# Four modulation vectors of the first block as row products on VectorE, and all later modulation issued after the first two heads' projections

## The chip, the core and the metric

The kernel runs on one core of one Trainium2 chip. A core has TensorE (PE, the matrix engine; its weight loads are PEld), VectorE (DVE), ScalarE (ACT), GpSimd (POOL) and SyncE (SP), which here issues most of the DMAs. Each engine works through its own instructions in order; engines wait for one another through semaphores. The metric is the device time of one execution in microseconds (us), as the median of the runs.

## The reference, cut to what matters

One transformer block with three mixers and a mixture of experts, then a second block of two layers. What the change touches is the modulation of the first block: `c` is one vector of 1024 numbers, and a 1024 x 6144 matrix turns it into six vectors.

```python
def first_block(x, c, ctx, c_ctx, w_mod, b_mod, ...):
    sc  = jax.nn.silu(c)                                  # (1, 1024)
    scc = jax.nn.silu(c_ctx)[None]
    mod_x = (sc @ w_mod + b_mod).reshape(-1, 6, 1024)     # six vectors for x
    mod_c = (scc @ w_mod[:, :2048] + b_mod[:2048])        # two for the context
    hx = modulate(rms_norm(x, g_mix), mod_x[:, 0], mod_x[:, 1])
    hc = modulate(rms_norm(ctx, g_mix), mod_c[0], mod_c[1])
    mx = hybrid_mixer(hx, hc, ...)                        # retention, window, neighbourhood
    x = x + mod_x[:, 2] * mx
    hx = modulate(rms_norm(x, g_ffn), mod_x[:, 3], mod_x[:, 4])
    x = x + mod_x[:, 5] * expert_choice_ffn(hx, ...)
# second_block: for each of two layers three more vectors, silu(c_2) @ mod_w_2[l] + mod_b_2[l],
# for x and for the context
```

Vectors 0 and 1 are wanted at once, 2 to 5 only behind the mixer. The vectors of the second block do not depend on the first and can be computed at any time.

## The kernel before

Activations lie as 128 channels by 512 tokens (256 for the context), eight tiles `hx` or `hc` for 1024 channels. A projection (`proj`) loads one 512 KB weight tile `wr` on SP's queue, splits it into a high part `wh` (a cast on ACT, L395) and a rest `wl` (a subtraction on DVE, L391), and multiplies three times (L404 to L406) over eight chunks, 24 matmuls in all. There are two buffers for `wr` and three each for `wh` and `wl`.

A modulation (`modblock`) goes in steps: a step loads a 512 KB tile `wm` and multiplies it by the silu vector, a stationary operand of 32 columns, with two matmuls of 512 columns (L471). 2048 columns take 16 steps; then four transposes (L480) turn the row into columns and DVE adds the bias (L486). `wmod0` (vectors 0 and 1) is drained at the start. `wmod1` and `wmod2` (vectors 2 to 5) and the second block's `mw1a` and `mw1b` (`mods2`, `mods2g`; 16 and 8 steps) follow through the generator `mods`, whose steps `pace` puts between those of the projections: one step for every PACE[i] units of projection cost, a projection being 5.2.

The stretch that the change touches is `block1_mixer` from the first retention projection on. `ret_proj(0)` projects heads 0 and 1 (four q and k projections with a rotary embedding on DVE, then the context's k, `v` for tokens and context, two gates). After its first projection the context `c` is loaded, squared and summed, and `hc` is normed and modulated. `ret_consts` computes the decay constants (`ls`, 24 tiny DVE instructions in a chain, then `lgs`). `ret_attn` makes for each head a strip `G` and a strip `CG` from them (`ret_strips`) and then goes over six key blocks: scores on PE, times the strip on DVE (the tile `A`, L832), `A` times v on PE (L834, L837). While it runs, `weave` fills in `ret_proj(1)` and later the first merge gates `G(0, 10)`, both with `mods` paced in. `drain(mods)` issues what is left, and the window attention follows.

The order on each engine is fixed when the kernel is built: a scheduler goes by the program order, the dependencies and its own idea of durations. Pools give the buffers: the tag `wbig` of pool `mr` has `s.nbig` buffers for modulation weights.

Of the kernel before, what the change touches and what calls it, by code (L numbers as in the profile page):

```python
# [7 lines left out]
F32 = mybir.dt.float32  # L8
# [7 lines left out]
D = 1024  # L16
# [127 lines left out]
def prep(i):  # L144
    f = {k: np.asarray(v) for k, v in i.items()}
    o = dict(_constants())
    o["xT"] = _tokT(f["x"][0])
    o["cT"] = _tokT(f["ctx"][0])
    o["cc"] = np.ascontiguousarray(np.stack([_cols(f["c"][0]), _cols(f["c_ctx"])], axis=-1))
    m = _modchunks(f["w_mod"][0])  # L150
    for n, a in enumerate(m):
        o[f"wmod{n}"] = a
    o["bmod"] = _cols(f["b_mod"][0])
    o["gmix"] = _cols(f["g_mix"][0])
    o["gffn"] = _cols(f["g_ffn"][0])
    o["gfin"] = _cols(f["g_final"])
    w = f["w_in"][0]
    off = {}
    at = 0
    for n, s in (("q_r", 512), ("k_r", 512), ("v_r", 512), ("g_r", 512), ("q_w", 512), ("k_w", 128), ("v_w", 128),  # L160
                 ("q_n", 512), ("k_n", 512), ("v_n", 512), ("gates", 3072)):
        off[n] = (at, s)
        at += s
    order = []

    def cols(n, a, m):
        return w[:, off[n][0] + a:off[n][0] + a + m]

    for h in (0, 256):
        order += [_tiles(cols(n, h, 256)) for n in ("q_r", "k_r")]  # L170
        order += [_vtiles(cols("v_r", h, 256)), _tiles(cols("g_r", h, 256))]
    order += [_tiles(cols("k_w", 0, 256)), _tiles(cols("q_w", 0, 512))]
    for h in (0, 256):
        order += [_tiles(np.concatenate([cols("q_n", h, 128), cols("k_n", h, 128)], axis=1)),
                  _vtiles(cols("v_n", h, 256)),
                  _tiles(np.concatenate([cols("q_n", h + 128, 128), cols("k_n", h + 128, 128)], axis=1))]
    order.append(_tiles(cols("gates", 0, 3072)))
    o["win"] = np.concatenate(order)
    o["lgt"] = _bcast(f["ret_decay_logit"][0])
    o["gn"] = _cols(f["ret_gn"][0])  # L180
    o["sink"] = _bcast(f["win_sink"][0])
    o["wbr"] = np.concatenate([_tiles(f["w_ret"][0]), _tiles(f["w_win"][0]), _tiles(f["w_na"][0])])
    o["wout"] = _tiles(f["w_out"][0])
    o["wrt"] = np.concatenate([f["w_router"][0], np.zeros((D, 16), np.float32)], axis=1).reshape(8, 128, 32).transpose(1, 0, 2)

    wg, wu, wd = [f[n][0].reshape(8, 2, 2, 4, 128, 2, 512).transpose(0, 5, 2, 1, 4, 3, 6)
                  for n in ("w_exp_gate", "w_exp_up", "w_exp_down")]
    o["wexp"] = np.concatenate([np.stack([wg, wu], axis=2).reshape(8, 16, 128, 2048), wd.reshape(8, 8, 128, 2048)],
                               axis=1)
    idx, ok = _na_index()  # L190
    rpb = f["na_rpb"][0]
    o["nab"] = np.stack([np.where(g[None], rpb[:, a[0], a[1]], np.float32(NEG)) for a, g in zip(idx, ok)], axis=1)
    _prep2(f, o)
    return {k: np.ascontiguousarray(v) for k, v in o.items()}
# [40 lines left out]
def drain(g):  # L235

    while True:
        try:
            next(g)
        except StopIteration as e:  # L240
            return e.value
# [40 lines left out]
def pace(main, extra, every):  # L282

    due = 0.0
    for c in main:
        yield c
        due += c
        while due >= every:
            due -= every
            c = next(extra, None)  # L290
            if c is not None:
                yield c
# [25 lines left out]
class Kern:  # L318
# [141 lines left out]
    def modblock(s, sc, src, width, dst, bias, col0, big=None, ps=None):  # L460

        nc = s.nc
        ps = s.mm() if ps is None else ps
        nj = width // 512
        for k in range(8):
            for j in range(nj):
                if j % 2 == 0:
                    w = s.wp.tile([128, 1024], F32, name=s.uid("wr"), tag="wraw", bufs=NRAW) if big is None else \
                        big.tile([128, 1024], F32, name=s.uid("wm"), tag="wbig", bufs=s.nbig)
                    nc.sync.dma_start(w, src[k][:, j * 512:j * 512 + 1024])  # L470
                nc.tensor.matmul(ps[32 * j:32 * j + 32, :], sc[:, k, :], w[:, j % 2 * 512:j % 2 * 512 + 512],  # L471
                                 start=k == 0, stop=k == 7)
                if j % 2:
                    yield 0.9
        n = 32 * nj
        rows = s.T(nm="mrow", tag="t5")
        nc.scalar.copy(rows[:n], ps[:n])
        pt = s.at()
        for i in range(4):
            nc.tensor.transpose(pt[:, i * 128:i * 128 + n], rows[:n, i * 128:i * 128 + 128],  # L480
                                s.const("ident")[:n, :n])
        pv = pt.rearrange("p (i j v) -> p j i v", i=4, j=4)
        for v in range(2):
            o = dst[:, v, col0:col0 + 4 * nj].rearrange("p (j i) -> p j i", j=nj)
            b = bias[:, col0:col0 + 4 * nj].rearrange("p (j i) -> p j i", j=nj)
            nc.vector.tensor_tensor(o, pv[:, 0:nj, :, v], b, ALU.add)  # L486
        yield 0.5


    def rstd_c(s, sq_sum, n, width, fold=None):  # L490
# [594 lines left out]
    def block1_mixer(s, xd, M, ctx2):  # L1085
# [18 lines left out]
        R = [{}, {}]  # L1104
        Y = []
        with s.pool("rp") as s.rp, s.pool("mr") as mr:
            s.nbig = 3
            pm = s.sc()
            bk = [pm[:, i * 512:i * 512 + 512] for i in range(3)]
            mods = itertools.chain(s.modblock(sc, s.d["wmod1"], 2048, mod, bm, 16, mr, bk[0]),  # L1110
                                   s.modblock(sc, s.d["wmod2"], 2048, mod, bm, 32, mr, bk[1]),
                                   s.mods2(1, M[1], mr, bk[2]), s.mods2g(1, M[1], mr, bk[0]))
            s.rdl, s.rcos, s.rsin = [s.pconst(s.rp, n) for n in ("dl", "cosr", "sinr")]
            g = s.ret_proj(0, R[0])
            next(g)
            c = s.loadx("cT", 256, "pj")
            qc = s.sqsum(c, 256)
            for _ in range(3):
                next(g)
                next(mods)  # L1120
            s.sc2 = s.silu2("cc2")
            rc = s.rstd_sb(qc, D, 256)
            s.hc = s.normmod(c, 256, A1[:, 1, :], mod[:, 1, 0:8], lambda: s.TT(256, "hc", "hc"), rc)
            drain(pace(g, mods, PACE[0]))
            s.ret_consts()
            fill.add(pace(s.ret_proj(1, R[1]), mods, PACE[1]))
            weave(s.ret_attn(0, R[0], Y), fill, 2.4)
            fill.flush()
            fill.add(pace(G(0, 10), mods, PACE[2]))
            weave(s.ret_attn(1, R[1], Y), fill, 1.8)  # L1130
            drain(mods)
# [965 lines left out]
    return {a: b if isinstance(b, (tuple, str)) else (b, w) for a, b in k.items()}  # L2097


PACE = (2, 2.5, 2.5)  # L2100
NEARLY = 20
NPRE = 44
LATE = True
# [98 lines left out]
```

## Time and profile before

| | us |
|---|---|
| median of 3 runs | 2881.63 (2880.66 to 2888.18) |
| the profiled execution, its own time | 2883.79 |
| its span, first to last instruction | 2882.0 |
| PE busy | 2717.6 (94%) |
| DVE busy | 1569.0 (54%) |
| ACT busy | 1230.7 (43%) |
| POOL busy | 144.5 (5%) |

How to read it: the span is that of the profiled execution; its own time is 1.8 us longer, and 2.2 us above the median. A share of busy time is a mean over stages. The change lies in the first 330 us, so that stretch is read by windows (busy time of each engine in a stretch), by the timeline (instructions in order of time, with the idle time before them and what ended it) and by the tiles concerned.

### The profile page before, as it was taken

Reading aid. Unit: us, or ns where it says so; the run is one execution under the profiler, and the core shown is the slowest. Engines: PE = TensorE matmul, PEld = TensorE weight load, DVE = VectorE, ACT = ScalarE, POOL = GpSimd, SP = SyncE. Lnnn points to the kernel's source line nnn. Section 1 sums busy time; section 2 is a strip of 40 time slices with the busy share of each in tenths; the row PEclk is TensorE's granted clock in tenths of the full one; section 3 lists DMA queues with packets and bytes.
Section 4 is the critical chain, followed back from the end, with each engine's and each line's share of the span. In section 5 each row is a group of like instructions: output and inputs, shape, how many; then the busy total and the mean of one; then the engine's idle time right before and its main releaser. Section 6 shows DMA issues by size and latency. Waiting matters only on the chain. (4 is left out here: it accounts for less than half of the span.)

```text
span 2882.0 us, 42045 instructions
## 1 busy us (share of the span) xinstructions
PE 2717.6 (94%) x16470; PEld 1889.2 (66%) x16470; DVE 1569.0 (54%) x2957; ACT 1230.7 (43%) x2159; POOL 144.5 (5%) x228
## 2 busy tenths in 40 slices
PE   6999999899969999999999899999999999989998
PEld 3666677787623555555555577777777777767776
DVE  3554676665442323455223656546866546746864
ACT  2333454354222214455212444445655544545652
POOL 1000001000001000000000000000010000000000
PEclk9999999999969999999999999999999999999998
DMA  8545425535789898888999532214354432114343
GB/s 281 174 168 183 145 77 178 189 103 198 263 315 356 304 331 295 316 286 295 321 331 333 189 113 78 72 39 141 115 181 135 131 116 89 50 34 140 117 159 120
DMA packets 170022, 537.68 MB, mean 187 GB/s; under 512 B 21784, under 2 KB 24936, under 8 KB 169824
## 3 DMA queue, kind: packets, MB, share of 16 engines
q1 hardware_dynamic: 141600, 462.50, 46.2%
q0 software_dynamic: 16128, 50.48, 5.3%
q10 hardware_dynamic: 12096, 22.03, 2.1%
q8 instruction: 129, 2.11, 0.3%
q14 instruction: 69, 0.57, 0.1%
HBM read 484.06 MB, written 48.76 MB: 185 GB/s over the span
## 5 line engine op out<-in xcount | busy, mean ns | idle before, releaser
L391 DVE TENSOR_TENSOR wl<-wr,wh 128x1024 fp32r<-128x1024 f32 x320 | 390.9, 1223 | 367.9 <-ACT wh L395 348.8
L395 ACT CAST wh<-wr 128x1024 fp32r<-128x1024 f32 x320 | 334.1, 1046 | 435.0 <-PE ps L405 355.0
L404 PE MATMUL ps<-hx,wh 128*128 128x512 f32 x1168 | 474.9, 407 | 12.8 <-ACT wh L395 7.7
L405 PE MATMUL ps<-hx,wh 128*128 128x512 f32 x1168 | 467.8, 401 | 0.0
L406 PE MATMUL ps<-hx,wl 128*128 128x512 f32 x1168 | 466.3, 400 | 0.6 <-DVE wl L391 0.5
L1301 PE MATMUL ps<-we,xe 128*64 128x512 f32 x1024 | 293.0, 609 | 5.0 <-DMA we<-in_wexp 4.9
L404 PEld LDWEIGHTS ps<-hx,wh 128*128 128x128 f32 x1168 | 221.4, 190 | 76.8 <-issue 12.4
L406 PEld LDWEIGHTS ps<-hx,wl 128*128 128x128 f32 x1168 | 220.9, 189 | 53.5 <-issue 5.0
L405 PEld LDWEIGHTS ps<-hx,wh 128*128 128x128 f32 x1168 | 221.4, 190 | 50.8 <-issue 6.4
L673 ACT ACTIVATE P<-ps,st 128x768 f32<-128x768 f32 (+3 forms) x144 | 111.0, 771 | 148.4 <-DVE st L669 113.6
L1301 PEld LDWEIGHTS ps<-we,xe 128*64 128x64 f32 x1024 | 77.8, 137 | 133.8 <-issue 107.8
L404 PE MATMUL ps<-hc,wh 128*128 128x256 f32 x496 | 145.1, 293 | 3.6 <-ACT wh L395 3.4
L406 PE MATMUL ps<-hc,wl 128*128 128x256 f32 x496 | 144.1, 291 | 0.2 <-DVE wl L391 0.2
L1301 PE MATMUL ps<-we,hT 128*64 128x512 f32 x512 | 139.9, 601 | 2.1 <-ACT hT L1341 1.6
L405 PE MATMUL ps<-hc,wh 128*128 128x256 f32 x496 | 140.2, 283 | 0.0
L667 DVE TENSOR_REDUCE st<-ps 128x1 f32<-128x768 f32 (+3 forms) x144 | 114.1, 793 | 40.7 <-PE ps L406 38.5
L695 PE MATMUL ps<-c_ident,P 128*128 128x128 f32 x688 | 112.0, 283 | 13.2 <-DVE P L678 6.4
L406 PEld LDWEIGHTS ps<-hc,wl 128*128 128x128 f32 x496 | 94.2, 190 | 28.2 <-issue 12.2
L695 PEld LDWEIGHTS ps<-c_ident,P 128*128 128x128 f32 x688 | 81.8, 143 | 46.8 <-ACT PT L698 14.2
L404 PEld LDWEIGHTS ps<-hc,wh 128*128 128x128 f32 x496 | 94.4, 191 | 26.8 <-issue 15.1
L698 ACT COPY PT<-ps 128x512 f32<-128x512 f32 x123 | 70.1, 586 | 88.5 <-PE ps L695 88.0
L471 PE MATMUL ps<-wm,sc_cc 128*32 128x512 f32 x384 | 88.1, 646 | 16.5 <-DMA wm<-in_wmod 16.5
(515 smaller groups left out, 5058.4 us busy)
## 6 DMA issues: line engine op xcount, KB each, us to landing
we<-in_wexp SPq DMA_DIRECT2D x384, 512.0 KB, 7.4
wr<-in_win SPq DMA_DIRECT2D x240, 512.0 KB, 3.8
wm<-in_wmod SPq DMA_DIRECT2D x48, 512.0 KB, 5.3
wr<-in_wbr SPq DMA_DIRECT2D x48, 512.0 KB, 3.5
dram<-th ACTq DMA_DIRECT2D x72, 256.0 KB, 2.1
mth<-dram SPq DMA_DIRECT2D x72, 256.0 KB, 5.0
wr<-in_wout SPq DMA_DIRECT2D x32, 512.0 KB, 4.2
dram<-mth POOLq DMA_DIRECT2D x48, 256.0 KB, 3.0
```

Source lines behind the costliest of these rows:

```text
L391: s.nc.vector.tensor_tensor(out, a, b, ALU.subtract)
L395: i = s.nc.scalar.copy(hi, src)
L404: t.matmul(out, a[0], b[0], start=start, stop=False)
L405: t.matmul(out, a[0], b[1], start=False, stop=False)
L406: t.matmul(out, a[1], b[0], start=False, stop=stop)
L471: nc.tensor.matmul(ps[32 * j:32 * j + 32, :], sc[:, k, :], w[:, j % 2 * 512:j % 2 * 512 + 512], start=k == 0, stop=k == 7)
L667: nc.vector.tensor_reduce(st[:, 0:1], sc[:, :n], AX.X, ALU.max)
L673: nc.scalar.activation(p[:, :n], sc[:, :n], AF.Exp, bias=st[:, 1:2], scale=scale, accum_out=st[:, 2:3])
L695: nc.tensor.transpose(tp[:, j:j + 128], blocks[(i + j) // 128], s.const("ident"))
L698: nc.scalar.copy(parts[i // 512][:, :m], tp[:, :m])
L1301: nc.tensor.matmul(ps[64 * e:64 * e + 64, :], stat[:, k, 64 * e:64 * e + 64], ws[e][:, kk * 512:kk * 512 + 512], start=k == 0, stop=k == 7)
```

## The change

- `prep` hands over `wmod1` and `wmod2` transposed as `wmodT`: 32 tiles of 128 output channels by 1024 inputs, the same bytes in the same number of DMAs. `crow` is `c` repeated over 128 partitions (512 KB).
- `silu_row` loads `crow` into a tile `row` on POOL's queue and takes twice its silu in place: two tanh on ACT, two `scalar_tensor_tensor` on DVE, each 128x512.
- `modrows` takes the place of the two `modblock`s: for each of the 32 tiles one DMA on SP's queue and one `scalar_tensor_tensor` on DVE of 128x1024, which multiplies the weight tile by 0.5 and by the row and sums along the row (`accum_out`) into one column of `mod`. One addition of the bias ends it. TensorE has no part in it.
- In `ret_proj(0)` no modulation is paced any more. The chain `mods` (row products, then `mods2`, `mods2g`) and the second block's `silu2` are issued behind it and behind `ret_consts`.
- `mr` has two `wbig` buffers instead of three, since `row` takes the room of one. PACE goes from (2, 2.5, 2.5) to (0, 1.8, 1.8).

```diff
@@ prep
-    for n, a in enumerate(m):
-        o[f"wmod{n}"] = a
+    o["wmod0"] = m[0]
+
+    o["wmodT"] = f["w_mod"][0][:, 2048:].T.reshape(32, 128, D)
+    o["crow"] = _bcast(f["c"][0])
@@ class Kern
+    def silu_row(s, pool, name):
+
+        nc = s.nc
+        r = pool.tile([128, D], F32, name=s.uid("row"), tag="row", bufs=1)
+        s.load(r, s.d[name])
+        for h in range(2):
+            x = r[:, h * 512:h * 512 + 512]
+            th = s.T(nm="rth")
+            nc.scalar.activation(th, x, AF.Tanh, scale=0.5)
+            nc.vector.scalar_tensor_tensor(x, th, 1.0, x, ALU.add, ALU.mult)
+        return r
+
+    def modrows(s, row, src, dst, bias, pool):
+
+        nc = s.nc
+        n = src.shape[0]
+        for t in range(n):
+            w = pool.tile([128, D], F32, name=s.uid("wt"), tag="wbig", bufs=2)
+            nc.sync.dma_start(w, src[t])
+            nc.vector.scalar_tensor_tensor(w, w, 0.5, row, ALU.mult, ALU.mult, accum_out=dst[:, t:t + 1])
+            yield 0.9
+        nc.vector.tensor_tensor(dst, dst, bias, ALU.add)
@@ block1_mixer
-            s.nbig = 3
+            s.nbig = 2
             pm = s.sc()
             bk = [pm[:, i * 512:i * 512 + 512] for i in range(3)]
-            mods = itertools.chain(s.modblock(sc, s.d["wmod1"], 2048, mod, bm, 16, mr, bk[0]),
-                                   s.modblock(sc, s.d["wmod2"], 2048, mod, bm, 32, mr, bk[1]),
-                                   s.mods2(1, M[1], mr, bk[2]), s.mods2g(1, M[1], mr, bk[0]))
@@ block1_mixer
             for _ in range(3):
                 next(g)
-                next(mods)
-            s.sc2 = s.silu2("cc2")
             rc = s.rstd_sb(qc, D, 256)
             s.hc = s.normmod(c, 256, A1[:, 1, :], mod[:, 1, 0:8], lambda: s.TT(256, "hc", "hc"), rc)
-            drain(pace(g, mods, PACE[0]))
+            drain(g)
             s.ret_consts()
+            s.sc2 = s.silu2("cc2")
+            row = s.silu_row(mr, "crow")
+            mods = itertools.chain(s.modrows(row, s.d["wmodT"], mod[:, 0, 16:48], bm[:, 16:48], mr),
+                                   s.mods2(1, M[1], mr, bk[2]), s.mods2g(1, M[1], mr, bk[0]))
-PACE = (2, 2.5, 2.5)
+PACE = (0, 1.8, 1.8)
```

In the pieces of order below, `wm` and `wt` are modulation weights, `qk` rotated queries and keys, `th_cc2` and `sc_cc2` the second block's silu; the numbers count tiles.

PE, before, just behind the first four q and k projections: the sums of the context's squares (L497, L533) and the first use of `hc`.

```order
L471 MATMUL ps68_289<-wm171_689,sc_cc_89 32x512 x2
L471 MATMUL ps68_289<-wm173_719,sc_cc_89 32x512 x2
L497 MATMUL ps123_515<-ones_69,sq85_346 128x1 x2
L471 MATMUL ps68_289<-wm174_723,sc_cc_89 32x512 x2
L533 MATMUL ps125_521<-c_ident_75,rs124_518 128x128 x2
L471 MATMUL ps68_289<-wm177_754,sc_cc_89 32x512 x2
L471 MATMUL ps68_289<-wm179_784,sc_cc_89 32x512 x2
L471 MATMUL ps68_289<-wm188_827,sc_cc_89 32x512 x2
L471 MATMUL ps68_289<-wm189_831,sc_cc_89 32x512 x2
L404 MATMUL ps155_581<-hc128_528,wh153_577 128x256
```

PE, after, at the same place.

```order
L408 MATMUL ps114_459<-hx64_277,wl113_456 128x512
L522 MATMUL ps120_495<-ones_69,sq85_346 128x1 x2
L558 MATMUL ps122_501<-c_ident_75,rs121_498 128x128 x2
L406 MATMUL ps152_561<-hc125_508,wh150_557 128x256
L406 MATMUL ps157_595<-hc125_508,wh155_591 128x256
L406 MATMUL ps164_634<-wh159_624,hx43_235 128x256
```

The modulation steps between the sums, the broadcast and the context's projections are gone; nine more matmuls of L471 that stood inside the first projection, ahead of its `wl`, are gone too.

DVE, before, where the decay constants begin: `gs196` is the first gate of the pair.

```order
L578 SCALAR_TENSOR_TENSOR gs196_896<-gs196_896,ps195_871 128x512
L736 TENSOR_SCALAR ls209_961<-ls208_960 128x8
L737 RECIPROCAL ls209_961<-ls209_961 128x8
L738 TENSOR_TENSOR ls210_962<-ls208_960,ls209_961 128x8
L739 TENSOR_TENSOR ls211_963<-ls210_962 128x8
```

DVE, after, at the same place: `gs188` is the second gate of the pair.

```order
L603 SCALAR_TENSOR_TENSOR gs188_870<-gs188_870,ps187_845 128x512
L761 TENSOR_SCALAR ls190_876<-ls189_875 128x8
L458 SCALAR_TENSOR_TENSOR th_cc2_919<-th_cc2_919,x_cc2_917 128x16
L393 TENSOR_TENSOR wl240_1087<-wr238_1084,wh239_1086 128x1024
L762 RECIPROCAL ls190_876<-ls190_876 128x8
L459 TENSOR_SCALAR sc_cc2_921<-th_cc2_919 128x8x2
L510 SCALAR_TENSOR_TENSOR wt287_1282,mod1_93<-wt287_1282,row195_925 128x1024
L763 TENSOR_TENSOR ls191_877<-ls189_875,ls190_876 128x8
L764 TENSOR_TENSOR ls192_878<-ls191_877 128x8
L767 TENSOR_TENSOR ls193_879<-ls193_879,ls192_878 128x8
L510 SCALAR_TENSOR_TENSOR wt288_1285,mod1_93<-wt288_1285,row195_925 128x1024
```

The chain now begins one gate later, and row products and two 128x1024 splits stand inside it: five products (L510) and two splits (L393) between `gs188` and the first `A` of head 0, where before there stood one split and no product.

PE, after, at the end of `mods`; `wm453` to `wm458` are the last six of the 24 steps for the second block, and `ps492` belongs to the window attention.

```order
L473 MATMUL ps68_289<-wm453_2118,sc_cc2_921 32x512 x2
L473 MATMUL ps68_289<-wm454_2122,sc_cc2_921 32x512 x2
L473 MATMUL ps68_289<-wm455_2126,sc_cc2_921 32x512 x2
L473 MATMUL ps68_289<-wm456_2130,sc_cc2_921 32x512 x2
L473 MATMUL ps68_289<-wm457_2134,sc_cc2_921 32x512 x2
L473 MATMUL ps68_289<-wm458_2138,sc_cc2_921 32x512 x2
L482 MATMUL ps460_2144<-c_ident_75,mrow459_2142 128x64 x4
L406 MATMUL ps492_2312<-hc125_508,wh490_2308 128x256
```

PE, before, a part of the same end: single steps between matmuls of the window's projections.

```order
L471 MATMUL ps68_289<-wm455_2163,sc_cc2_511 32x512 x2
L405 MATMUL ps469_2220<-hx59_266,wh467_2216 128x512
L406 MATMUL ps469_2220<-hx58_265,wl468_2217 128x512
L404 MATMUL ps469_2220<-hx61_271,wh467_2216 128x512
L471 MATMUL ps68_289<-wm456_2167,sc_cc2_511 32x512 x2
```

Six steps now stand in one run with nothing between them, and they share two buffers.

## Rows read from the trace of the kernel before

**Rows 1.** The page, busy time, share of the span and instructions of an engine

```profile
PE 2717.6 (94%) x16470; PEld 1889.2 (66%) x16470; DVE 1569.0 (54%) x2957; ACT 1230.7 (43%) x2159; POOL 144.5 (5%) x228
```

**Rows 2.** Windows: stretch, length; PE, PEld, DVE, ACT, POOL busy; clock; DMA share, GB/s

```profile
77.00:94.50 17.50, 10.79 (x42) 2.63 (x40) 16.84 (x36) 8.33 (x16) 0.00 (x0) 0.72 0.70 240
...
217.00:296.00 79.00, 79.00 (x329) 50.34 (x327) 35.51 (x49) 25.98 (x35) 2.12 (x4) 1.00 0.55 187
```

**Rows 3.** Windows of the tile wm alone (L471): PE busy and records

```profile
94.50:217.00 122.50, 15.50 (x82) 2.40 (x80) 0.98 0.46 159
217.00:296.00 79.00, 11.43 (x64) 1.73 (x64) 1.00 0.55 187
296.00:313.00 17.00, 8.03 (x32) 1.33 (x32) 1.00 0.72 253
```

**Rows 4.** Timeline of PE: start, us, instruction, idle before it and what ended it

```profile
55.98 0.63 PE L404 MATMUL ps<-hx,wh 128*128 128x512 f32 x1
56.40 0.63 PE L405 MATMUL ps<-hx,wh 128*128 128x512 f32 x1
...
58.07 0.39 PE L404 MATMUL ps<-hx,wh 128*128 128x512 f32 x1
58.30 0.39 PE L405 MATMUL ps<-hx,wh 128*128 128x512 f32 x1
...
92.64 1.92 PE L471 MATMUL ps<-wm,sc_cc 128*32 128x512 f32 x4 [2.69 <-DMA wm<-in_wmod]
...
170.28 1.02 PE L837 MATMUL ps<-A,vc 128*128 128x512 f32 x2
...
185.77 1.05 PE L471 MATMUL ps<-wm,sc_cc 128*32 128x512 f32 x4 [1.40 <-DMA wm<-in_wmod]
```

**Rows 5.** Timeline of SP's DMA issues

```profile
45.64 6.50 SPq L470 DMA_DIRECT2D wm<-in_wmod  x4
52.23 0.86 SPq L412 DMA_DIRECT2D wr<-in_win  x2
...
65.43 1.85 SPq L1081 DMA_DIRECT2D c<-in_cT  x4
```

**Rows 6.** Timeline of DVE and ACT, first and last of the context's norm; first late cast

```profile
59.09 1.05 ACT L395 CAST wh<-wr 128x1024 fp32r<-128x1024 f32 x1 [10.03 <-DMA wr<-in_win]
...
86.77 0.88 DVE L567 SCALAR_TENSOR_TENSOR nf<-c,A,rb 128x256 f32<-128x256 f32 x2
...
91.92 2.06 DVE L570 SCALAR_TENSOR_TENSOR hc<-nf,mod,hc 128x256 fp32r<-128x256 f32 x5
```

**Rows 7.** Groups by line and shape: busy, mean ns, idle before

```profile
L391 DVE TENSOR_TENSOR wl<-wr,wh 128x1024 fp32r<-128x1024 f32 x320 | 390.9, 1223 | 367.9 <-ACT wh L395 348.8 <-PE ps L837 6.5 <-PE ps L406 5.4
L567 DVE SCALAR_TENSOR_TENSOR nf<-c,A,rb 128x256 f32<-128x256 f32 x24 | 10.6, 479 | 0.0
L567 DVE SCALAR_TENSOR_TENSOR nf<-x,A,rb 128x512 f32<-128x512 f32 x8 | 5.8, 748 | 0.0
L673 ACT ACTIVATION_READ_ACCUMULATOR P<-ps,st 128x1 f32 x144 | 27.9, 194 | 0.0
```

**Rows 8.** Timeline of DVE from the decay constants to the first A of head 0

```profile
130.21 0.17 DVE L736 TENSOR_SCALAR ls<-ls 128x8 f32<-128x8 f32 x1
...
136.44 0.68 DVE L578 SCALAR_TENSOR_TENSOR gs<-gs,ps 128x512 f32<-128x512 f32 x1
...
138.03 1.22 DVE L391 TENSOR_TENSOR wl<-wr,wh 128x1024 fp32r<-128x1024 f32 x1
...
140.74 0.69 DVE L832 SCALAR_TENSOR_TENSOR A<-ps,G 128x512 f32<-128x512 f32 x1
```

**Rows 9.** Timeline of DVE, the first A of head 1 behind head 0's reciprocal

```profile
180.46 3.35 DVE L849 RECIPROCAL sq<-sq 128x512 f32<-128x512 f32 x1 [0.99 <-ACT sq L848]
183.72 0.63 DVE L832 SCALAR_TENSOR_TENSOR A<-ps,G 128x512 f32<-128x512 f32 x1
```

**Rows 10.** DMA issues: KB each, median us from issue to landing

```profile
wm<-in_mw1b SPq DMA_DIRECT2D x8, 512.0 KB, 4.1
```

## The prediction

> **What bounds the kernel now.** The page is read first: PE is busy 2717.6 of 2882.0 us, DVE little more than half [rows 1]. That is a mean, and the change touches only the first 330 us; from the window attention on, the order of both kernels is the same, so what is gained or lost there is shifted to the end unchanged. So the windows of the first stretch come next. From 217 to 296 PE is busy 79.00 of 79 us at the full granted clock [rows 2]. From 94.5 on its timeline shows one wait only, 1.40 us at 185.77 for a modulation tile [rows 4]. Between 77 and 94.5 it is busy 10.79 of 17.5 us at a granted clock of 0.72 [rows 2]: there it waits. Hence each modulation step that leaves PE behind 94.5 is worth its own length, unless something else comes late; and all idle time that the change makes behind 94.5 is lost.
>
> In each step below the sum is made against the profiled execution, 2883.79 us, which lies 2.2 above the median of 2881.63. A matmul of 512 columns follows another after 0.23 us at the full clock, and after 0.42 at the lower level (58.07 to 58.30, and 55.98 to 56.40 [rows 4]). So a projection of 24 takes 5.5 us and a score of three 0.7.
>
> **Term 1, the steps that leave PE.** L471 is 15.5 us busy from 94.5 to 217 [rows 3]. With the change no modulation matmul stands there until the second gate of the next pair of heads (one of the next pair's first steps aside). Two rounds of transposes go too, 0.4 each by the row's spacing, and the wait of 1.40. Together -17.6, with little doubt (-16 to -18).
>
> **Term 2, the front.** SP issues the first `wr` at 52.23, behind four `wm` that took 6.50 from 45.64 [rows 5]; the cast of a `wr` at 59.09 had waited 10.03 us for it [rows 6]. With the change these four `wm` are gone from ahead of `wr`. Up to 6.5 us can be won for the first projections; the context `c`, issued at 65.43 [rows 5], and the rotary work between move up with them, and I take 4.2 of it as arriving at `hc`, since the norm also hangs on DVE's other work. Then, before, the context's projections began only behind the steps at 92.64, which had waited 2.69 for `wm` and ended at 94.56 [rows 4], when the last `hc` was done (91.92 + 2.06 = 93.98 [rows 6]). With the steps gone, they run while `hc` arrives: some 61 matmuls of 256 columns, half of 0.23 each, 7.3 us. Together -11.5. The end towards nothing: the two `row` products stand between the `hc` on DVE, and -4 is left; the other end is -14.
>
> **Term 3, the first A of head 0.** Before, the decay chain began at 130.21, after the *first* gate, and the first `A` began at 140.74 and ended at 141.43, 11.2 us later, with one split of 1.22 between [rows 8]; PE was then in the middle of other projections and did not wait. With the change the chain begins after the *second* gate. Call the end of that gate's matmuls T. The activation, and ACT's part ahead of the chain, which stands behind it on ACT, take some 2.4 us (estimate from 0.68 for DVE's gate op [rows 8] and as much again for each ACT step). Then the chain: 11.2 less the split and the second gate's op, 1.22 + 0.68 (both stood inside it before), 9.3. Inside it stand now two splits, 2.4, and five row products. No product is in the trace. The nearest rows are `scalar_tensor_tensor` over 512 columns from two SBUF tiles, 748 ns, over 256 columns, 479 ns, and the 1024 columns of a split, 1223 ns [rows 7]; extended by the difference of the first two, 1024 columns cost 1.29, and I take 1.3. The lower end is 1.22; the sum into a column may add something like ACT's 194 ns for reading a sum [rows 7], and the upper end, should the sum halve the rate, is 2.6. Five are 6.5. With 0.4 for the waits between, A is ready at T + 21. PE has by then only one projection and two scores to do, 5.5 + 1.4 = 6.9, before it wants A; then it stands. So +14. The two ends: 0, if A is ready within 6.9; +20, with products at the upper end. The products wait for their DMAs too, and on DVE's queue everything behind them waits along: the splits, the gates, the chain. With two buffers a product's DMA goes out when the product two ahead is done and lands some 4.1 us later [rows 10], so two come in 5.4 us. By that the five fit into the 21 us.
>
> **Term 4, later A of head 0.** The scores behind the rotary work on DVE are as short of cover, and products stand in between: +3 (0 to 6).
>
> **Term 5, the first A of head 1.** Before, head 0's last A v product on PE began at 170.28 [rows 4], and head 1's first A ended at 183.72 + 0.63, behind the normalization of head 0 with a reciprocal of 3.35 [rows 9]: 13.1 us from 171.3. PE had modulation steps and the context's projections to fill it. With the change two or three products, an extra split and the rounding of `y` stand on the way, some 2.6 + 1.2 + 2.8, and it comes to 19.7; PE has then 8 to 10 us of work: two scores, the context's key projection (24 of 0.12) and the like. +9 (0 to 13).
>
> **Term 6, the clock.** The granted clock is 1.00 when PE is full and was 0.72 where it was busy 10.79 of 17.5 us [rows 2]. The idle stretches of terms 3 and 5 are of that kind. A matmul at the lower level costs 0.19 us more; some 20 of them, +4 (0 to 6).
>
> **Term 7, the end of the modulation.** The second block's 24 steps took 11.43 + 8.03 = 19.5 us before (96 records, four to a step [rows 3]) and were spread out with three buffers. With the change row products have come first, so 24 steps remain when the third phase begins, and the last six stand in one run. There, with two buffers, each pair waits for the pair ahead to leave its buffers and for the landing of 4.1 [rows 10], beside 1.05 for a step [rows 4]: three rounds of 5.1 instead of 6.3 for six, +9; in the others nearer to each other than before another +2.6, and +1.5 for the clock behind it. +13 (0 to 16).
>
> **The sum.** -17.6 - 11.5 + 14 + 3 + 9 + 4 + 13 = +13.9: 2897.7 for an execution like the profiled one, less 2.2, 2895.
>
> **The rivals.** *Head 0's strip is in time* (the other side). If A is ready within 6.9 us of T, PE does not stand, the clock stays, and terms 3 to 6 vanish: -17.6 - 11.5 + 13 = -16.1, 2866. For it: the chain's inputs are constants, and DVE was busy 35.51 of 79 us [rows 2]. Against it: the chain alone needed 11.2 us [rows 8], and it stands in fixed order behind the second gate. It decides at T + 6.9. Chance 0.12. *One stall serves for all.* While PE stands for head 0, DVE, ACT and the DMAs get ahead; then terms 4, 5 and 6 are gone: -17.6 - 11.5 + 14 + 13 = -2.1, 2880, no change. For it: the queues run ahead of PE. Against it: head 1's A hangs on head 0's last A v through a chain, whatever was ready earlier. 0.23. *The product at half rate.* If a product with its sum takes 2.6, eleven or twelve of them on the way of terms 2 to 5 cost 1.3 more each, some +15: 2910. For it: no row shows a sum on DVE. Against it: without one, 512 columns from two SBUF tiles take 748 ns where the simpler split takes 1223 for 1024 [rows 7], so two sources alone do not double the time. 0.15. [...] *The steps don't leave*: the work is still on PE, or the waits for weight tiles take their place on SP's queue, where a product's DMA holds the next `wr` back, so that terms 1 and 2 go and little else comes: 2882. Against it: the order shows the steps gone. 0.05.
>
> **How the numbers follow.** The forecast has 0.45. A measurement of this kernel tells about 0.3%, 8.6 us, from no change: faster is below 2873.0, slower above 2890.3. Of the forecast's 0.45, whose own range is 2884 to 2906, 0.36 lies above 2890.3 and 0.09 within. The rival at 2866 gives 0.12 faster; that at 2880, 0.03 faster, 0.18 same, 0.02 slower; that at 2910, 0.15 slower; the last, 0.01 faster and 0.04 same. Sum: 0.16 faster, 0.31 same, 0.53 slower. The range leaves out the rival at 2866 and the tail of the one at 2910: 2872 to 2914.
>
> **What would show it.** In the changed kernel's profile: records of L471 down by 128; the context's key projections done some 11 us earlier; the second gate's op on DVE near 122 instead of 136.44 [rows 8]; PE idle some 14 us before the first A v of head 0, ended by DVE's A, and some 9 before that of head 1; a product at 1.3 us; the last six steps of the second block's modulation in one run with waits for `wm` from the DMA; the end of the modulation some 14 us later. The forecast is wrong if the stalls before A are below 8 us in sum, if the product is far from 1.3, or if the six steps find their tiles landed.

## The result, and the profile after

The changed kernel takes 2907.4 us (median of 4 runs, 2906.4 to 2910.3) against 2881.1 for the kernel before: 1.0088 of its time, 95% interval 1.0070 to 1.0105. The forecast was 2895, slower, in a range of 2872 to 2914. The profiled execution took 2906.4, 22.6 us more than that of before; the sum had said 13.9. The medians differ by 26.3: the profiled execution of the kernel before lies 2.7 above its median of 2881.1, that of the changed kernel 1.0 below its own.

The page of the changed kernel, the span and the row that answers to [rows 1]: PE is busy 13 us less and has 136 instructions fewer (128 matmuls of L471 and eight transposes), and the span is 23 us longer.

```profile
span 2904.6 us, 41861 instructions
...
PE 2704.5 (93%) x16334; PEld 1890.7 (65%) x16334; DVE 1605.5 (55%) x3020; ACT 1231.2 (42%) x2159; POOL 144.7 (5%) x229
```

Where the time went is read off by landmarks: the same piece of work in both timelines of PE, and the difference of its times.

| on PE | before, us | after, us | difference |
|---|---|---|---|
| context's key projections end | 102.86 | 92.47 | -10.4 |
| second gate of heads 0 and 1 ends | 134.90 | 121.27 | -13.6 |
| first A v of head 0 begins | 143.19 | 143.52 | +0.3 |
| first gate of heads 2 and 3 begins | 216.43 | 220.63 | +4.2 |
| window attention's first transposes begin | 321.78 | 342.96 | +21.2 |
| the last of its transposes of v begins | 324.3 | 349.3 | +25.0 |
| last of the program's landmarks | 2793.5 | 2816.5 | +23.0 |

Up to 121 us the change wins 13.6. It then loses 18 between the second gate and the next pair's gate, and 21 more up to the last of the window's transposes of v. Behind that nothing is won back or lost: the difference stays at 21 to 26 us over 2400 us.

The windows of the changed kernel, columns as in [rows 2]. From 120 to 217 PE is busy 72.44 of 97 us at a granted clock of 0.86; before it was busy all but 1.4 of them at 1.00. In the last window the clock is 0.81.

```profile
77.00:94.50 17.50, 11.37 (x69) 10.71 (x70) 15.45 (x31) 10.05 (x18) 0.00 (x0) 0.71 0.12 42
94.50:120.00 25.50, 25.35 (x173) 23.45 (x173) 16.97 (x24) 8.07 (x13) 0.00 (x0) 1.00 0.77 265
120.00:217.00 97.00, 72.44 (x332) 54.38 (x331) 79.89 (x149) 29.14 (x42) 0.00 (x0) 0.86 0.52 181
217.00:296.00 79.00, 78.97 (x323) 51.42 (x322) 36.02 (x45) 28.73 (x38) 2.12 (x4) 1.00 0.47 161
296.00:350.00 54.00, 43.19 (x185) 23.40 (x184) 19.65 (x32) 13.88 (x21) 0.00 (x0) 0.81 0.48 161
```

What PE waited for between 118 and 343 us, from the view of waits (us in total, times, longest): one wait makes up nearly half.

```profile
PE ps L859 <- DVE A L857: 17.8, 3, 15.4
PE ps L406 <- DVE kc L393: 6.6, 1, 6.6
PE ps L473 <- DMA wm<-in_mw1b: 5.6, 6, 1.9
PE ps L406 <- DVE r L751: 4.0, 1, 4.0
PE ps L482 <- ACT mrow L479: 0.7, 1, 0.7
PE ps L473 <- DMA wm<-in_mw1a: 0.6, 2, 0.4
```

The 15.4 in DVE's timeline: it begins with the second gate's op and the first link of the decay chain and ends with head 0's first A; of the five products between, the first and the last stand here. From 125.07 to 142.69, 17.6 us, DVE had five products, two splits and the chain with its strips; PE stood from 128.07 to 143.52.

```profile
125.07 0.68 DVE L603 SCALAR_TENSOR_TENSOR gs<-gs,ps 128x512 f32<-128x512 f32 x1
125.67 0.16 DVE L761 TENSOR_SCALAR ls<-ls 128x8 f32<-128x8 f32 x1
...
127.73 1.23 DVE L510 SCALAR_TENSOR_TENSOR wt<-wt,row 128x1024 f32<-128x1024 f32 x1 [0.54 <-DMA wt<-in_wmodT]
128.88 0.08 DVE L510 DVE_READ_ACCUMULATOR wt<-wt,row 128x1 f32 x1
...
141.55 1.21 DVE L510 SCALAR_TENSOR_TENSOR wt<-wt,row 128x1024 f32<-128x1024 f32 x1
142.69 0.08 DVE L510 DVE_READ_ACCUMULATOR wt<-wt,row 128x1 f32 x1
142.69 0.68 DVE L857 SCALAR_TENSOR_TENSOR A<-ps,G 128x512 f32<-128x512 f32 x1
```

The other loss is seen in PE's timeline at the end of the modulation. Six steps stand in a row and each waits for its tile; from 326.92 on a step takes 1.9 us instead of 1.05. Behind the last comes a wait of 4.01 that the forecast did not have.

```profile
322.27 1.05 PE L473 MATMUL ps<-wm,sc_cc 128*32 128x512 f32 x4 [0.57 <-DMA wm<-in_mw1b]
323.96 1.05 PE L473 MATMUL ps<-wm,sc_cc 128*32 128x512 f32 x4 [0.64 <-DMA wm<-in_mw1b]
326.92 1.87 PE L473 MATMUL ps<-wm,sc_cc 128*32 128x512 f32 x4 [1.91 <-DMA wm<-in_mw1b]
329.63 1.92 PE L473 MATMUL ps<-wm,sc_cc 128*32 128x512 f32 x4 [0.84 <-DMA wm<-in_mw1b]
...
337.67 0.69 PE L482 MATMUL ps<-c_ident,mrow 64*128 64x64 f32 x4 [0.68 <-ACT mrow L479]
342.37 0.58 PE L406 MATMUL ps<-hc,wh 128*128 128x256 f32 x1 [4.01 <-DVE r L751]
```

DVE at the same place says why: the rotary embedding of the window's first key (L746 to L752) stands behind the bias of the modulation's last vectors (L488), which waits 14.58 us for the transposes; and PE's next projection waits for the rotary work.

```profile
338.39 0.24 DVE L488 TENSOR_TENSOR mod<-ps,c_mb 128x8 f32<-128x8 f32 x2 [14.58 <-PE ps L482]
...
338.82 0.68 DVE L746 TENSOR_TENSOR r<-ps,pc 128x512 f32<-128x512 f32 x1
...
341.62 0.69 DVE L751 TENSOR_TENSOR r<-ps,pc 32x512 f32<-32x512 f32 x1
```

### The profile page after: what moved, and what is told of

The parts are those of the page before. It is cut to its first block, busy times and chain, and to the rows that moved or that the text cites. A ratio compares the mean times of both kernels' runs of the same rounds, so it can differ in the third digit from the quotient of the medians.

```text
span 2904.6 us, 41861 instructions
## 1 busy us (share of the span) xinstructions
PE 2704.5 (93%) x16334; PEld 1890.7 (65%) x16334; DVE 1605.5 (55%) x3020; ACT 1231.2 (42%) x2159; POOL 144.7 (5%) x229
## 5 line engine op out<-in xcount | busy, mean ns | idle before, releaser
L393 DVE TENSOR_TENSOR wl<-wr,wh 128x1024 fp32r<-128x1024 f32 x320 | 390.6, 1222 | 331.4 <-ACT wh L397 312.9
L720 PE MATMUL ps<-c_ident,P 128*128 128x128 f32 x688 | 112.4, 283 | 13.2 <-DVE P L703 6.3
L406 PEld LDWEIGHTS ps<-hc,wh 128*128 128x128 f32 x496 | 95.4, 193 | 36.0 <-issue 14.6
L720 PEld LDWEIGHTS ps<-c_ident,P 128*128 128x128 f32 x688 | 81.9, 143 | 47.7 <-ACT PT L723 15.4
L407 PEld LDWEIGHTS ps<-hc,wh 128*128 128x128 f32 x496 | 95.6, 193 | 5.0 <-issue 4.6
```

What stands on the lines that cost most here:

```text
L393: s.nc.vector.tensor_tensor(out, a, b, ALU.subtract)
L406: t.matmul(out, a[0], b[0], start=start, stop=False)
L407: t.matmul(out, a[0], b[1], start=False, stop=False)
L720: nc.tensor.transpose(tp[:, j:j + 128], blocks[(i + j) // 128], s.const("ident"))
```

## The experiments

Ratios are against the kernel before, measured beside each run, with 95% intervals.

**Decay constants asked for earlier.** One call is moved:

```diff
             s.hc = s.normmod(c, 256, A1[:, 1, :], mod[:, 1, 0:8], ...)
+            s.ret_consts()
             drain(g)
-            s.ret_consts()
```

> The changed kernel with one call moved: the decay constants are asked for right behind hc's norm, ahead of the context's key projections, instead of behind the second gate. Theory (the stall before head 0's first A, 15.45 us of PE idle in the changed kernel's trace, comes from the chain's place behind the second gate): that idle falls below 3 us and with it the restarts at the lower clock, so the time falls from 2907 to about 2889. Rival (VectorE is full of row products, the wait only moves to the weight splits and gates behind them): the stretch from the second gate on wins less than 6 us and the time stays above 2900.

Measured: 2894.4 us, 1.0036 (1.0017 to 1.0054); 13 us less than the changed kernel, 5 more than expected. PE's wait before head 0's first A is gone, 0 instead of 15.45. On DVE that A now stands ahead of the second gate's op:

```profile
123.30 0.69 DVE L857 SCALAR_TENSOR_TENSOR A<-ps,G 128x512 f32<-128x512 f32 x1
123.91 0.68 DVE L603 SCALAR_TENSOR_TENSOR gs<-gs,ps 128x512 f32<-128x512 f32 x1
```

The gate of heads 2 and 3 begins at 206.97 instead of 220.63, 13.7 earlier. The products are all still there, so it was the chain's place, behind the second gate and with products inside, that PE paid for. The other waits did not move to take its place, nor did they shrink: 1.49, 6.63 and 0.89 us before the later A, against 1.49, 6.64 and 0.89 in the changed kernel. One new one came, 1.36 for rotary work.

**Three buffers.** The 1 KB that lacks for a third comes from the silu operand of the first modulation:

```diff
-        sc = s.silu2("cc")
...
         with s.pool("bigA") as big:
             s.nbig = 7
+            sc = s.silu2("cc", big)
...
-            s.nbig = 2
+            s.nbig = 3
```

(and `bufs=3` in `modrows`).

> The changed kernel with three buffers for modulation weights again, for row products and second-block steps alike; the 1 KB that lacks for it comes from the silu operand of the first modulation, which is put into the pool of that modulation. Theory (the end of the modulation, 17 us later against the rest than before, comes from two buffers): the last eight steps no longer stand in one run, the waits for wm from 303 us on (about 7 us in sum), the 4.0 us wait behind them and the lower clock of 0.81 in 296 to 350 go, and the time falls from 2907 to about 2891; the 15.45 us before head 0's first A stay. Rival (the late steps are bound by their DMAs whatever the buffers): the same waits, above 2903.

> Both edits together: decay constants ahead, three buffers. Theory: the two losses are in different stretches and add up, so 2907 less 18 less 16, about 2873, which is below the kernel before (2881) by the 8 to 12 us that PE no longer spends on the steps. Rival (what one takes away the other gives back, since row products on VectorE are the cause): 2885 to 2900.

Measured: three buffers alone 2895.3, 1.0055 (1.0035 to 1.0076); both edits 2887.0, 1.0023 (1.0010 to 1.0036). The steps of the second block stand singly between other matmuls, as expected. What the buffers are worth is best read between the two kernels that have the early constants: from the gate of heads 2 and 3 to the last transposes of v it took 129.2 us with two buffers (206.97 to 336.2), 115.4 with three (210.62 to 326.0), and 107.9 in the kernel before (216.43 to 324.3). So 13.8 of the 21 us of that stretch are the buffers; the other 7.5 stay, and the waits of 1.55 for a `wm` and 2.90 for rotary work that are left there account for 4.5 of them. With three buffers alone the scheduler put some steps ahead of the gate, where they waited 7.6 us in sum.

Both edits together came out 14 us above what the theory gave, at the rival's time, but only in part for the rival's reason: of the five waits below, those of 1.49, 6.65 and 0.89 stood in the changed kernel already, and the two for rotary work, 4.1 us, are new. These are the waits in PE's timeline of the kernel with both edits, 130 to 184 us:

```profile
142.43 0.51 PE L406 MATMUL ps<-qk,kc 128*128 128x512 f32 x1 [2.45 <-DVE r L751]
144.89 3.47 PE L859 MATMUL ps<-A,v 128*128 128x512 f32 x4 [1.49 <-DVE A L857]
167.03 0.38 PE L406 MATMUL ps<-hc,wh 128*128 128x256 f32 x1 [1.61 <-DVE r L751]
176.82 0.80 PE L406 MATMUL ps<-qk,qk 128*128 128x512 f32 x1 [6.65 <-DVE kc L393]
179.36 3.67 PE L859 MATMUL ps<-A,v 128*128 128x512 f32 x4 [0.89 <-DVE A L857]
```

13 us remain there that neither edit was made for; the expectation had counted the steps that left PE as a gain and forgotten terms 4 and 5 of the prediction.

**The operand at its old place.** Both edits had also shifted the start: PE's first projection began at 42.89 instead of 40.23. The pool of the first modulation is opened ahead of `x`, so that `silu2("cc", big)` stands first again.

> The run with both edits once more, with the pool of the first modulation opened ahead of x, so that its silu operand stands at its old place in program order. In the run with both edits the first projection began at 42.9 us instead of 40.2, and hc came 3 us later. Theory: this is the operand's new place, the 3 us come back: about 3 us below the run with both edits. Rival (the later start is chance of the DMAs): the same as the run with both edits.

Measured: 2884.8, 1.0005 (0.9996 to 1.0014); the gate of heads 2 and 3 begins at 207.18 instead of 210.62, so at that landmark the 3.4 us are back. The first projection begins at 40.79. The times alone would not show it: the intervals of the two kernels overlap.

**The order without the products.** The four vectors by `modblock` on PE again, all else as changed:

```diff
-            mods = itertools.chain(s.modrows(row, s.d["wmodT"], ...),
+            mods = itertools.chain(s.modblock(sc, s.d["wmod1"], 2048, mod, bm, 16, mr, bk[0]),
+                                   s.modblock(sc, s.d["wmod2"], 2048, mod, bm, 32, mr, bk[1]),
```

> The order and the buffers of the change without its row products: the four vectors are computed on TensorE by the old steps, but all this behind the first two heads' projections in program order, with two buffers and the changed kernel's pace. Theory (place of the chain, order and two buffers cost the time, not the arithmetic on VectorE): no better than the kernel before, 2885 to 2915, with the wait for head 0's first A short because its chain has no products and splits inside. Rival (the products on VectorE cost the time): close to the kernel before, 2876 to 2884.

Measured: 2932.6, 1.0186 (1.0165 to 1.0206), above both expectations. In this order and with two buffers the products are worth some 25 us; the rival is out. The chain has no products and one split inside; on DVE from the second gate's op to A it takes 10.1 us instead of 17.6:

```profile
124.24 0.68 DVE L601 SCALAR_TENSOR_TENSOR gs<-gs,ps 128x512 f32<-128x512 f32 x1
...
134.29 0.68 DVE L855 SCALAR_TENSOR_TENSOR A<-ps,G 128x512 f32<-128x512 f32 x1
```

So 7.6 of the 17.6 are what was put inside the chain. The other 10 are the gate's op (0.6), the tiny instructions (4.9), the strips (3.4) and the one split (1.1). Counted from the end of the second gate's matmuls, 122.20 here, A is ready after 12.8 us, where the changed kernel needs 22.1, and in both PE's next projection and two scores end 6.8 us after the gate. By that, an estimate, 6 of the 15.45 us belong to the chain's place behind the second gate and 9 to the products and splits. In this run PE spends these 6 on three steps, 2.1 us, and on a wait of 3.90 for a `wm`, so that its wait for A itself is 0.17. And the waits of PE from 120 to 217 us show that the wait for `kc`, 6.6 in the changed kernel, does not come from the products:

```profile
PE ps L404 <- DVE kc L391: 5.7, 1, 5.7
PE ps L471 <- DMA wm<-in_wmod: 5.5, 2, 3.9
PE ps L857 <- DVE A L855: 1.6, 3, 0.9
```

**The wait for kc.** A score of head 1 waits on PE for the split of `kc`, and on DVE that split stands behind head 0's reciprocal of 3.35 us. With the pace of before, on the kernel with the operand at its place, the split comes ahead:

```diff
-PACE = (0, 1.8, 1.8)
+PACE = (0, 2.5, 2.5)
```

> The same, with a modulation step for every 2.5 units of projection in the second and third phase, as the kernel before has it, instead of 1.8. On DVE the split of kc then stands ahead of head 0's reciprocal of 3.35 us, as in the kernel before. Theory (the 6.6 us that PE waits for kc before head 1 in all runs so far come from that place in DVE's order): that wait falls below 2 us, the last seven steps of the modulation stand in one run and cost 2 to 4 us of waits: 2872 to 2878 if the kernel before is at 2881. Rival (head 1 waits for its chain anyhow): the wait only changes its name, 2880 or more.

Measured: 2883.9, 1.0012 (1.0003 to 1.0021). The wait for `kc` falls from 6.67 to 1.86, and the window from 120 to 217 has 90.29 us of work instead of 84.40, as the theory has it. DVE's order there:

```profile
165.16 0.42 DVE L393 TENSOR_TENSOR kc<-ps,kc 128x256 fp32r<-128x256 f32 x1
166.63 3.35 DVE L874 RECIPROCAL sq<-sq 128x512 f32<-128x512 f32 x1
169.89 0.63 DVE L857 SCALAR_TENSOR_TENSOR A<-ps,G 128x512 f32<-128x512 f32 x1
```

The time missed the expected 2872 to 2878 and lies where the rival had it, though no other wait took the place of the 6.67; the price at the end was too low: the last steps in one run cost 10.6 us of waits (1.78, 1.58, 1.39, 0.68 and 5.15, the last again for the rotary work), not 2 to 4.

**The products in the order of before.** `row` and `mods` made ahead of `ret_proj(0)`, paced in from its start, PACE 2, 2.5, 2.5, three buffers; then the same with the early constants.

```diff
+            row = s.silu_row(mr, "crow")
+            mods = itertools.chain(s.modrows(row, s.d["wmodT"], ...), ...)
             g = s.ret_proj(0, R[0])
...
-            drain(g)
+            drain(pace(g, mods, PACE[0]))
```

> The row products alone, in the order of the kernel before: paced into the first two heads' projections from their start, pace 2, 2.5, 2.5, three buffers, decay constants asked for where they were. Theory (the products are cheap where DVE has room; what costs is a chain with products inside it that PE waits for): here too the chain comes behind the second gate with seven products and two splits from the gate to the first A, so head 0's first A has PE wait 10 to 16 us again, and the time is 2880 to 2895. Rival (the change's new order does the damage): no such wait, 2865 to 2872.

> The row products in the order of the kernel before, three buffers, and the decay constants asked for behind hc's norm. Theory: no wait before head 0's first A; the steps that left PE (about 31 us of 32 steps, of which some 14 were ahead of 94.5 us where PE waits anyway) are a gain: 2866 to 2876 if the kernel before is at 2881. Rival (row products in the first projections hold back the splits and the DMAs of the first weights): the context's projections end later than in the changed kernel (93.6 us) by 5 us or more, 2880 or more.

Measured: 2884.2, 1.0004 (0.9995 to 1.0013), and with the early constants 2874.9, 0.9974 (0.9962 to 0.9986). The first has PE wait 11.39 us ahead of head 0's first A, for a `wm` whose DMA stood behind those of the products on SP (issued at 139.02); the A itself ended on DVE only at 145.8, 1.9 us behind that wait, so the chain would have held PE as long. With the chain out of the way the kernel is faster than the one before. Both expectations of time held. But the rival's sign is there too: with the early constants the context's key projections end at 97.9 us, 5 later than in the changed kernel, and on DVE five products stand ahead of and among the norm's instructions for `hc` (83.42 to 96.58 us).

**What the runs point to.** Products asked for only behind `hc` and the constants, paced 2, 2.5, 2.5, three buffers, the operand at its place:

```diff
             s.hc = s.normmod(...)
             s.ret_consts()
+            s.sc2 = s.silu2("cc2")
+            row = s.silu_row(mr, "crow")
+            mods = itertools.chain(s.modrows(...), s.mods2(...), s.mods2g(...))
-            drain(g)
+            drain(pace(g, mods, PACE[0]))
...
+PACE = (2, 2.5, 2.5)
```

> The row products with what the runs so far say of each loss: products asked for only behind hc's norm and the decay constants (as in the run with both edits and the operand at its place), then paced 2, 2.5, 2.5 as in the kernel before, three buffers. On DVE kc's split stands ahead of head 0's reciprocal, no product stands ahead of hc, and the second block's last steps stand one by one between the window's matmuls. Theory: the context's projections end near 93 us (as in the changed kernel, not 98 as where products come earlier), no wait above 3 us from there to the window attention, and the window attention begins 12 to 18 us earlier than in the kernel before: 2864 to 2872 if that is at 2882. Rival (PE is bound by splits and DMAs of weights once the steps are gone, so that any order lands at the same time): 2873 to 2880.

> The same with a pace of 3, 2.5, 2: the products begin more sparsely and the second block's steps come closer together in the third phase. Theory (with three buffers and single steps the pace hardly matters): within 4 us of the run with 2, 2.5, 2.5. Rival (steps that come closer wait for their DMAs): slower by 5 to 10 us, with waits for wm from the DMA behind 290 us.

Measured: 2873.3, 0.9958 (0.9942 to 0.9975), and with the pace 3, 2.5, 2 2875.1, 0.9961 (0.9948 to 0.9974): faster than the kernel before by 11 us, 0.4%, and than the changed kernel by some 35; the pace hardly matters, as expected. The windows of the first, columns as in [rows 2], where the changed kernel had 72.44, 78.97 and 43.19:

```profile
120.00:217.00 97.00, 90.26 (x435) 68.35 (x434) 81.97 (x120) 38.67 (x51) 0.00 (x0) 0.95 0.60 200
217.00:296.00 79.00, 79.00 (x315) 45.99 (x313) 31.81 (x42) 22.43 (x29) 2.12 (x4) 1.00 0.62 202
296.00:350.00 54.00, 52.96 (x274) 40.94 (x273) 41.02 (x76) 26.31 (x47) 0.00 (x0) 1.00 0.34 111
```

The window attention's first transposes begin 11.6 us earlier than in the kernel before, just short of the 12 to 18 expected, and one wait is above the 3 us allowed: 3.58 before head 1's first A, which stands right behind the reciprocal on DVE (169.37 to 172.71). The time, 2873.3, lies outside the 2864 to 2872 expected and in the rival's 2873 to 2880. The rival, that any order lands at the same time once the steps are gone, is not excluded for the best kernels: the one with the products in the order of before and the early constants, 0.9974, has an interval that overlaps these two. What is shown is that all three are faster than the kernel before; that the last order is better than the one ahead of it is not.

## Why the prediction was right, and where its sizes were off

The sign and the two places of the losses were right; the sum was 8.7 us too low for the profiled execution, and the medians moved by 26.3 where 13.4 was forecast. The range held, but it is 42 us wide and has no change within it, so the terms say more than the number. Point by point, to the gate of heads 2 and 3 (+0.9 predicted, +4.2 measured) and from there to the last of the window's transposes of v (+13 predicted, +20.8 measured):

*Term 1*, -17.6: no modulation matmul stands between 94.5 and 217 in the changed kernel, and its 15.5 us of [rows 3] are gone. With that the rival in which the steps don't leave is out.

*Term 2*, -11.5: the context's key projections end 10.4 earlier. The last `hc` is written at 91.01 instead of 93.98, 3.0 earlier where 4.2 was taken, and the other 7.4 are PE working while `hc` arrives, as worked out: its first matmul on `hc` begins at 83.16 instead of 94.49. One reading in this term was wrong: the `wr` issued at 52.23 is not the first but the third. Two had gone out from 28.05 on, and a buffer comes free for the third only when the first is split, at 50.10. So the four `wm` could hold it back by 2.1 us and not by 6.5; in the changed kernel it goes out at 49.25, when the first split has ended at 49.17.

*Term 3*, +14: 15.45, by the mechanism told. The chain from T, 121.27, to A's end at 143.37 took 22.1 where 21 was worked out, PE's cover 6.8 where 6.9 was, so the rival with head 0's strip in time is out. The experiment with the early constants shows the cause, and the one without products its two parts. A sign was missed by little: the second gate's op came at 125.07, not near 122, since two products and a wait of 1.55 for the first one's tile stand ahead of it on DVE.

*The price of a product*, 1.3: the group's row has a mean of 1221 ns, and reading the sum is an instruction of its own.

```profile
L510 DVE SCALAR_TENSOR_TENSOR wt<-wt,row 128x1024 f32<-128x1024 f32 x32 | 38.8, 1221 | 16.3 <-DMA wt<-in_wmodT 16.1
```

The same line's own view, for the second instruction (ns: least, median, most; first and last start in us):

```profile
L510 DVE DVE_READ_ACCUMULATOR wt<-wt,row x32: 78/81/85, 92.8 to 210.5; 128x1 f32 x32
```

Together 1.3, as taken, and the 1.22 alone are the time of a split of the same size [rows 7]. The rival of the product at half rate is out: no run shows a product of 2.6, which was a supposition, and two tiles of 1024 columns in SBUF, multiplied and summed along the row, took 1221 ns where the subtraction of two such tiles takes 1223 [rows 7]. Of the wait for the products' tiles, 16.1 us of DVE's idle time in 11 waits, three fall in the 22.1, with 2.65 us (1.55, 0.54 and 0.56) where 0.4 was taken.

*Terms 4 and 5*, +3 and +9: 1.5 and 7.5. Term 5's own numbers, 19.7 less 8 to 10, give 9.7 to 11.7 and not 9. That head 1's was of about the right size is luck, for the reason was not the one given: PE stood at a score, for the split of `kc` that stands behind the reciprocal, and only 0.9 of it at A itself. The run without products has 5.7 of it all the same.

*Term 6*, the clock, +4, was too small: 7.8 are left of the 4.2 when the waits and terms 1 and 2 are taken out (4.2 + 17.6 + 10.4 - 15.4 - 1.5 - 7.5). Most of that is seen directly: behind the wait of 15.45 the granted clock was 0.50 from 143.5 to 149.5 us, behind that of 6.64 it was 0.51 from 185.9 to 194, and PE was busy 13.2 us in these two stretches. At 1.00 that work would have taken half as long, so the clock cost 6.6: an estimate from the two clocks, beside which stand the spacings of matmuls of 512 columns, 0.43 us behind the first wait (147.07 to 147.50) and 0.23 later (150.04 to 150.27). Behind the wait of 1.49 the clock was 1.00, from 157.6 to 165. The other 1.2 of the 7.8 stay open. The groups of A v between 120 and 217 us, after and before (us busy, mean ns | idle):

```profile
L859 PE MATMUL ps<-A,v 128*128 128x512 f32 x16 | 10.9, 793 | 17.8 <-DVE A L857 17.8
```

```profile
L834 PE MATMUL ps<-A,v 128*128 128x512 f32 x16 | 8.3, 598 | 0.0
```

The 24 matmuls behind head 0's first A v took 8.2 us (144.58 to 152.76), 2.7 more than 5.5. Some 20 matmuls of 0.19 were counted for both stalls together; the first alone cost as much as 14 of them.

*Term 7*, +13, is the term that was mis-sized: 20.8. Six steps in one run waiting for tiles were foreseen, and their waits, 5.6 us, are less than the 9 given. Two things were missed: from the third of them on they took 1.9 us instead of 1.05, at a granted clock of 0.51 from 326.9 to 337 where it was 1.00 from 322.3 to 325, and the window's rotary embedding waits on DVE behind the bias that ends the modulation, 4.0. The latter is read from DVE's order and was not tested by itself, but the other traces agree with it. In the seven runs in which that bias waited 14.4 to 22.1 us on DVE (two or three buffers, steps in one run or singly), PE waited 2.9 to 5.2 for the rotary work behind it; where the bias waited 10.1 (pace 3, 2.5, 2), PE waited 1.4, and in the three where it waited 3.9 to 4.6, 0.4 or less. With the slower steps, 3.4 us, and the wait of 0.68 ahead of the transposes, 13.7 of the 20.8 are named; matmuls behind the wait of 4.01 that follow one another after 0.21 us instead of 0.12, at a granted clock of 0.50 from 342.4 to 347.4, add some 2, an estimate, and the rest stays open. The modulation ended 26 us later (its last transposes at 337.67 against 311.66), not 14. Three buffers took 13.8 of the stretch away.

*The rival in which one stall serves for all* is out: behind the first stall PE still waited 9.0 us, and taking the first away left these three waits as they were to within 0.01 us. *That the difference only shifts behind the window attention* holds: it stays between 21 and 26 us to the end.

## What to carry to other kernels

Work taken off the busiest engine wins only what that engine does not then wait for: here the work moved to DVE stood inside a chain there that the busy engine waited for, and the chain itself had moved behind the last work that covered it. That the modulation steps had also been filler between such waits is shown only in small, by the three steps in the run without products. Before such a move, look on the engine that gets the work for chains that the busy engine waits for, ask for these first, and let the new work in behind them. A buffer given up for the move has to be priced where the buffers are used last, not where the move is.

## What was not expected of the hardware

In the changed kernel the two longest stalls of PE between the second gate and the next gate, 15.45 and 6.64 us, cost more than their length: beside the 24.5 us of waits there stand some 6.6 us more, by the estimate above, in matmuls at granted clocks of 0.50 and 0.51 behind these two. In the stretch at the end the granted clock was 0.73 from 313 to 343 us: the steps behind waits of 0.57 and 0.64 us still took 1.05 us, the one behind 1.91 took 1.87, and the three after it, behind 0.76 to 0.84, took 1.92.

The gain of the best kernel is larger at the window attention than some executions show at the end: in its profiled one the landmark at 1616 us is 9.5 us earlier than before and that at 2584 us 5.5, with the same order of PE's matmuls in both. Its six runs reach from 2864.6 to 2881.5; what sets this spread, beyond 1600 us, stays open.
